# A fused two-layer encoder on one core: `wo`'s third block in a spare bank, and a new order of sums, root and keys ahead of the cross-attention

## The chip, the cores and the metric

The kernel runs on one core of a Trainium2 chip, in one launch. The metric is the device time of that core in microseconds. An engine takes its instructions in the order of its own queue; the order is fixed when the program is built. TensorE (PE) multiplies, VectorE (DVE) and ScalarE (ACT) do the element work, SyncE (SP) and GpSimd (POOL) start the transfers.

## The reference

Two layers over a sequence of 512 tokens of width 1024, in float32. Each layer is a mixer, a cross-attention to a memory of 256 tokens, and a gated feed-forward; the change touches the seam between the mixer and the cross-attention.

```
for layer in range(2):
    xn = rms_norm(x, mix_norm[layer])
    mixed = fox_diff_mixer(xn, ...)  if layer == 0 else  mlstm_mixer(xn, ...)
    x = x + mixed                                   # ends in "@ w_out"
    x = x + memory_cross_attention(rms_norm(x, xattn_norm[layer]), rms_norm(mem, mem_norm[layer]), wq, wkv, wo)
    x = x + conv_ffn(rms_norm(x, ffn_norm[layer]), ...)
return rms_norm(x, final_norm)

def memory_cross_attention(xn, memn, wq, wkv, wo):  # 4 heads of 256
    q = split_heads(xn @ wq, 4)
    k, v = jnp.split(memn @ wkv, 2, axis=-1)
    p = jax.nn.softmax((q @ k^T) * 256 ** -0.5)
    return merge_heads(p @ v) @ wo
```

## The kernel before

**Products.** Every float32 product is done in three: each operand is split into a high half (a cast on ScalarE, line 285) and a low half (a subtraction on VectorE, line 282), and TensorE adds high x high, high x low and low x high (lines 291 to 293). A weight block comes by DMA into `raw` (or another buffer) and becomes `wh`, `wl`.

**The order.** Each stage is planned by a small list planner (`Plan`): items have a priority, the items they depend on, resources they take and free, an estimated time, and optional order marks (`order`) that only say "behind that item". It writes the program in the order found, and the framework below then fixes the order on each engine. PSUM has eight banks: four "acc" banks and two rings of two, "s" (small results) and "w" (aux: weighings, transposes, first query products).

**The mixer's output projection** (`p_out`): eight blocks `m` of 128 output rows; each takes an "acc" bank, does 8 x 3 products of 512 columns against the heads' outputs (`mh`/`ml`, and in layer 0 the last heads' `ka`, `qa`), and is then added to `x` (`xadd`, line 619). `xprep` makes `xh`, `xl` of the new `x` (lines 603, 604) and adds its square to `sq` (lines 597, 598). In layer 0 two of the four "acc" banks are held at that time by the fills, so the blocks pass through the other two. In that layer `x` is loaded again for the add (`reload`).

**The fills** (`p_fill`): the first four blocks of the memory's keys are multiplied early into two "acc" banks; their results are scaled later (`keys`, line 1372) and split into `kv`.

**The queries** (`p_query`, one call for each head `h` of four) use seven products of 256 columns in place of eight (a fast two-by-two scheme). `p_forms` makes sums and differences of `x`'s parts (lines 1495 to 1498, into `kv`); the weights' sums are made partly by DMA: `sum_load` loads one part into `sa` (line 1169, SP), then an accumulating DMA on POOL adds the other (line 1170). `sa` has three buffers, so the fourth sum, head 3's, is loaded once `wl<-sa` of head 0 has been read off the first. `rest_load` loads `ra`. Inside `p_query`, `p6` makes the sum `sa + raw` on VectorE (line 1228) into `sb` or `qs`, splits it as `s2` and multiplies; `p3` adds the other half of `raw` (line 1239); `p4` splits `ra`. For heads 0 and 1 these items have priorities of their own, interleaved with the end of the output projection; `seed` copies -X into the accumulating bank (line 1214), `kept` copies intermediate results to `xe` tiles (line 1224).

**The norm of the queries** is applied in the softmax: `rsqrt_cols` sums `sq` over the partitions with eight small matmuls (line 452, into an "s" bank), and `rsqrt` takes the root's inverse in twelve small VectorE steps (lines 461 to 467). The first score needs the result as the exponential's scale. The `xe` tiles (four buffers) also hold the exponentials.

Of the kernel before, what the change touches and what calls it, by code (L numbers as in the profile page):

```python
# [17 lines left out]
P = 128  # L18
SEQ = 512
DM = 1024  # L20
KB8 = DM // P
MEM = 256
# [5 lines left out]
EPS = 1e-6  # L28
# [108 lines left out]
MM = 0.2275  # L137
# [99 lines left out]
class Builder:  # L237
# [64 lines left out]
            self.mm3(ps[:, :n], wh[:, s], wl[:, s], xh[k][:, :n], xl[k][:, :n], k == 0, k == nk - 1)  # L302
        return ps

    def p_proj(self, pl, src, xs, evac, chain, deps=(), kdeps=None, edeps=(), prio=None, n=SEQ, nk=KB8, order=None, etake=(), per=2, eorder=(), load=(), off=0):

        order = order or list(range(nk))
        st = {}
        last = None
        cuts = list(range(0, nk, per)) + ([nk - 1] if per == 2 and nk > 6 else [])  # L310
        for c, e in zip(cuts, cuts[1:] + [nk]):
            ks = order[c:e]

            def fn(c=c, ks=ks):
                if c == 0:
                    st["w"] = self.weight(src, nk * P, off)
                    st["ps"] = self.acc_bank(st["banks"][0])
                (wh, wl), (xh, xl) = st["w"], xs()
                for j, k in enumerate(ks):
                    s = slice(k * P, (k + 1) * P)  # L320
                    self.mm3(st["ps"][:, :n], wh[:, s], wl[:, s], xh[k][:, :n], xl[k][:, :n], c + j == 0, c + j == nk - 1)

            d = list(deps) if c == 0 else [last]
            for k in ks:
                d += (kdeps or {}).get(k, [])
            first = c == 0
            last = pl.add(
                fn, 3 * len(ks) * MM * n / 512, d, prio, take=("acc", "wt") if first else (), free=("wt",) if e == nk else (),
                pre=(("A", 0.12 * nk), ("D", 0.14 * nk)) if first else (), st=st,
            )  # L330
        return pl.add(lambda: evac(st["ps"]), 0, [last, *edeps], prio, take=etake, free=("acc",), chain=chain, order=eorder, load=load, st=st)

    def p_proj_tok(self, pl, src, xs, ntok, evac, deps=(), kdeps=None, edeps=(), prio=None, n=512, etake=(), ready=None, chain=None):

# [88 lines left out]
    def xs(self):  # L423
        return self.xh, self.xl

    def p_out(self, pl, src, mixed, kdeps, gain, gi, order, prio, reload=False, order0=None):

        state = {}
        done = []
        for m in range(KB8):  # L430
            e = self.p_proj(
                pl, src[m], mixed, lambda ps, m=m: self.xadd(m, ps, reload), (("D", 0.6),), kdeps=kdeps, order=order, prio=prio + m
            )
            done.append(
                pl.add(lambda m=m: self.xprep(m, gain, gi, state), 0, [e], prio + m, chain=(("A", 0.52), ("D", 0.66), ("A", 0.52)), order=[order0])
            )
        self.state = state
        self.xdone = {k: [d] for k, d in enumerate(done)}
# [167 lines left out]
    def xprep(self, k, gain, gi, state):  # L606

        if gain is not None:
            if k == 0:
                self.xh, self.xl = [None] * 8, [None] * 8  # L610
            self.xh[k] = self.til(self.xp, f"xh{k}", dtype=F32R, bufs=1)
            self.xl[k] = self.til(self.xp, f"xl{k}", dtype=F32R, bufs=1)
            self.gained(k, self.x[k][:], self.col(gain, gi * 8 + k), self.xh[k][:], self.xl[k][:])
        self.squares(k, self.x[k][:], SEQ, state)

    def xadd(self, m, ps, reload=False):
        if reload:
# [559 lines left out]
    def p_query(self, pl, layer, h, order):  # L1177
# [3 lines left out]
        st = {}  # L1181
        a1, a2 = self.t["xq"][layer, 2 * h], self.t["xq"][layer, 2 * h + 1]

        def wide(tag, raw):
            both = self.til(self.kp, tag, (P, 1088), F32R, bufs=1)
            s = st[tag] = [both[:, c : c + 512] for c in (OFF, OFF + 512)]
            self.split(*s, raw)

        def product(w, c, xs, bank, first, ks=range(4)):
            for k in ks:  # L1190
                at = slice(c + k * P, c + (k + 1) * P)
                self.mm3(st[bank][:, :256], w[0][:, at], w[1][:, at], *xs(k), first and k == 0, k == 3, True)
# [31 lines left out]
            nc.scalar.copy(st[n][:], st[bank][:, :256])  # L1224

        def p6():
            st["sb"] = self.til(mp, "qs", bufs=1) if h % 2 else self.til(self.kp, "sb", bufs=2)
            tt_(out=st["sb"][:], in0=self.sums[h][:, 512:], in1=st["raw"][:, :512], op=ALU.add)
            if h == 0:
                self.sum_load(layer, 2)  # L1230
            wide("s2", st["sb"][:])
            product(st["s2"], 0, T2, "Y", False, range(4 - (h == 0)))
# [18 lines left out]
        n = 1.42  # L1251
# [15 lines left out]
        pl, mp, fin, ends = yield sd  # L1267
# [3 lines left out]
        formed = self.formed[1:] if lead else self.formed  # L1271
        q5 = pl.add(p5, n - part, formed, p5a, take=("s", "wt"))
        q6 = pl.add(p6, n - part, [sd, *formed], p6a, order=[q5])
        if lead:
            q5 = pl.add(lambda: product(st["f1"], 512, T1, "R", True, range(3, 4)), part, [q5, *self.formed], p5_, order=[q6])
# [12 lines left out]
    def xattn(self, layer):  # L1288
        nc, t, tc = self.nc, self.t, self.tc
        with tc.tile_pool(name=f"xa{layer}", bufs=1, reuse_waits="tile") as mp:  # L1290
            self.mp = mp
            pl = Plan(self.plan, [st["banks"][0] for st in [*self.fills, *self.held]], s=2, w=0, e=4, q=2, pt=2, wt=1, hs=2)
# [13 lines left out]
            def last():  # L1306
# [5 lines left out]
            self.formed.insert(0, pl.add(  # L1312
                last, 0, self.xdone[7], 0, order=self.formed[:], take=("hs", "hs"), free=("hs", "hs")
            ))
            norm = pl.add(
                lambda state=self.state: rs.append(self.rsqrt_cols(state["sq"], SEQ, 256.0 / DM, 256.0 * EPS)), 0.4, self.xdone[7], 2.5, take=("s",), free=("s",), chain=(("D", 2.3),)
            )
            mh, ml = [None] * 8, [None] * 8
            kd = {}
            kth, ktl, vh, vl, rs = [], [], [], [], []  # L1320
            qs, qe = [None] * 4, [None] * 4
# [43 lines left out]
            for h in range(4):  # L1365
                p = 50 + 10 * h
                ke = []
                for m in (2 * h, 2 * h + 1):

                    def keys(ps, m=m, at=0):  # L1370
                        tmp = self.til(mp, "tmp", (P, MEM))
                        nc.vector.tensor_tensor(out=tmp[:], in0=ps[:, at : at + MEM], in1=self.memrb, op=ALU.mult)
                        self.split(kth[m // 4][:, m % 4, :], ktl[m // 4][:, m % 4, :], tmp[:])

                    kc = (("D", 0.34), ("A", 0.34), ("D", 0.34))
                    if m < 2 * len(self.fills):
                        st = self.fills[m // 2]
                        ke.append(
                            pl.add(
                                lambda keys=keys, st=st, m=m: keys(st["ps"], at=m % 2 * MEM), 0, [kvs], p, free=("acc",) if m % 2 else (), chain=kc, st=st,  # L1380
                                order=ke[-1:] if m % 2 else (),
                            )
                        )
                        continue
                    ke.append(
                        self.p_proj(
                            pl, t["xk"][layer, m], self.mems, keys, kc, deps=[kvs], prio=p, n=MEM, per=4, off=OFF
                        )
                    )
# [85 lines left out]
            for k in range(4):  # L1475
                last_form = pl.add(
                    lambda k=k: form(k), 0, [*used, *self.xdone[2 * k + 1]], 100 + 2 * k + 2, order=[last_form],
                    chain=(("A", 1.5), ("D", 1.4), ("A", 1.0), ("D", 1.2)) if k < 3 else (),
# [817 lines left out]
```

## Time and profile before

| | before |
|---|---|
| median of 3 runs | 1459.03 us (1458.19 to 1459.31) |
| profiled execution | 1458.72 us |
| its span | 1456.9 us, TensorE clock 0.999 |
| PE busy | 1440.6 us (99%), 9019 instructions |
| DVE busy | 1225.9 us (84%) |
| ACT busy | 985.5 us (68%) |
| POOL busy | 72.9 us (5%) |
| DMA | 190.24 MB, 131 GB/s over the span |

A row of the timeline shows the start, the duration, the engine, the line, the operation, out<-in by the program's names, and in brackets the idle time ahead of it and what ended it. Matmuls overlap: a row's duration is longer than the distance to the next start, which is the pace. The profile's line numbers are those of the kernel before; in the changed kernel they are one to five higher. The seam lies at about 220 to 335 us of the span in layer 0 and 935 to 1040 us in layer 1.

### The profile page before, as it was taken

How to read it: one execution, taken by the hardware profiler on the slowest of the kernel's cores; microseconds unless marked ns; L12 is line 12 of the kernel's file. 1: busy time of each engine (PE TensorE's matmuls, PEld its weight loads, DVE VectorE, ACT ScalarE, POOL GpSimd, SP SyncE). 2: the span in 40 equal slices, each digit the busy share in tenths (PEclk: the TensorE clock that was granted, in tenths of full speed). 3: DMA queues.
4: the chain of work that ended last, by engine and by line, in shares of the span. 5: the costliest groups of instructions: out<-in, count | busy, mean ns of one | idle time of the engine just before them, and what ended most of it. 6: DMA issues, size and time to landing. Idle time of an engine off the chain costs nothing.

```text
span 1456.9 us, 24068 instructions
## 1 busy us (share of the span) xinstructions
PE 1440.6 (99%) x9019; PEld 1277.7 (88%) x9019; DVE 1225.9 (84%) x2224; ACT 985.5 (68%) x1775; POOL 72.9 (5%) x116
## 2 busy tenths in 40 slices
PE   9999999999999999999999999999999999999998
PEld 7888787998899999999888888889988999999987
DVE  7789987867899988889669988887779998888974
ACT  7689665655677777777547665566566777777764
POOL 0001120000000000000000100000000000000000
PEclk9999999999999999999999999999999999999999
DMA  5222436652246656662233332656413666656322
GB/s 200 87 74 73 118 122 195 169 179 87 94 122 169 183 158 157 155 160 77 84 101 108 111 109 65 204 142 189 131 49 117 162 178 173 154 157 160 104 67 78
DMA packets 70628, 190.24 MB, mean 131 GB/s; under 512 B 7520, under 2 KB 7520, under 8 KB 70512
## 3 DMA queue, kind: packets, MB, share of 16 engines
q1 hardware_dynamic: 62304, 161.38, 35.0%
q0 software_dynamic: 7200, 26.22, 10.6%
q8 instruction: 70, 1.15, 0.3%
q10 hardware_dynamic: 1008, 1.12, 0.2%
q14 instruction: 46, 0.38, 0.1%
HBM read 186.56 MB, written 2.13 MB: 130 GB/s over the span
## 4 chain that ended last, share of the span: by engine, by line
PE 82%; DVE 10%; ACT 4%; issue 2%; DMA 2%; SPq 0%; POOL 0%; ACTq 0%; DVEq 0%; POOLq 0%
PE acc L291 15%; PE acc L292 14%; PE acc L293 14%; PE w L293 6%; PE w L291 6%; PE w L292 6%; PE s L293 3%; PE s L291 3%; PE s L292 3%; PE acc L352 2%; PE acc L354 2%; PE acc L353 2%; DVE wl L282 2%; DMA sa<-in_xq_dram 1%; DVE x L771 1%
## 5 line engine op out<-in xcount | busy, mean ns | idle before, releaser
L282 DVE TENSOR_TENSOR wl<-raw,wh 128x1024 fp32r<-128x1024 f32 (+3 forms) x181 | 213.9, 1182 | 41.2 <-ACT wh L285 32.4
L291 PE MATMUL acc<-xh,wh 128*128 128x256 f32 (+1 forms) x624 | 206.8, 331 | 0.2 <-ACT v L1917 0.2
L293 PE MATMUL acc<-xh,wl 128*128 128x256 f32 (+1 forms) x624 | 205.6, 329 | 0.1
L292 PE MATMUL acc<-xl,wh 128*128 128x256 f32 (+1 forms) x624 | 205.5, 329 | 0.0
L285 ACT CAST wh<-raw 128x1024 fp32r<-128x1024 f32 (+1 forms) x123 | 126.6, 1034 | 84.3 <-PE acc L292 42.9
L1676 DVE SCALAR_TENSOR_TENSOR c<-hs,vec,c 128x512 f32<-128x512 f32 x176 | 130.4, 749 | 16.0 <-ACT c L1669 14.0
L291 PEld LDWEIGHTS acc<-xh,wh 128*128 128x128 f32 x624 | 117.2, 188 | 12.1 <-ACT v L1917 0.6
L293 PEld LDWEIGHTS acc<-xh,wl 128*128 128x128 f32 x624 | 117.2, 188 | 12.0 <-DVE wl L282 0.5
L292 PEld LDWEIGHTS acc<-xl,wh 128*128 128x128 f32 x624 | 117.2, 188 | 11.5
L293 PE MATMUL w<-ah,wl 128*128 128x512 f32 x304 | 119.1, 392 | 0.0
L292 PE MATMUL w<-al,wh 128*128 128x512 f32 x304 | 118.6, 390 | 0.0
L291 PE MATMUL w<-ah,wh 128*128 128x512 f32 x304 | 118.5, 390 | 0.0
L282 DVE TENSOR_TENSOR wl<-sa,wh 128x1024 fp32r<-128x1024 f32 x52 | 63.6, 1222 | 17.0 <-ACT wh L1747 15.6
L1669 ACT ACTIVATE c<-hs,vec 128x512 f32<-128x512 f32 x88 | 71.2, 816 | 9.6 <-DVE hs L1816 8.2
L1747 ACT CAST wh<-sa 128x1024 fp32r<-128x1024 f32 x42 | 44.0, 1049 | 35.5 <-PE w L292 30.5
L293 PEld LDWEIGHTS w<-ah,wl 128*128 128x128 f32 x304 | 57.1, 188 | 12.1
L291 PEld LDWEIGHTS w<-ah,wh 128*128 128x128 f32 x304 | 57.1, 188 | 10.1 <-ACT w L1584 0.2
L292 PEld LDWEIGHTS w<-al,wh 128*128 128x128 f32 x304 | 57.1, 188 | 9.8
L282 DVE TENSOR_TENSOR s<-sb,s 128x512 fp32r<-128x512 f32 x92 | 63.1, 686 | 2.2 <-ACT s L285 0.3
L1554 ACT CAST wh<-dr 128x512 fp32r<-128x512 f32 x64 | 39.7, 621 | 34.2 <-PE w L292 32.2
L1732 POOL DMA_DIRECT2D sa<-in_up_dram x42 | 35.9, 855 | 516.5 <-DVE wl L282 184.5
L291 PE MATMUL acc<-mem,wh 128*128 128x256 f32 (+1 forms) x192 | 61.5, 320 | 0.0
(535 smaller groups left out, 4664.1 us busy)
## 6 DMA issues: line engine op xcount, KB each, us to landing
raw<-in_up_dram SPq DMA_DIRECT2D x46, 512.0 KB, 3.4
sa<-in_up_dram SPq DMA_DIRECT2D x42, 512.0 KB, 4.1
sa<-in_up_dram POOLq DMA_DIRECT2D x42, 512.0 KB, 5.5
dr<-in_down_dram SPq DMA_DIRECT2D x64, 256.0 KB, 2.8
ra<-in_up_dram SPq DMA_DIRECT2D x42, 256.0 KB, 3.1
raw<-in_xk_dram SPq DMA_DIRECT2D x16, 512.0 KB, 3.6
raw<-in_wo_dram SPq DMA_DIRECT2D x16, 512.0 KB, 3.6
raw<-in_xv_dram SPq DMA_DIRECT2D x16, 512.0 KB, 3.4
```

Of the source, the lines that this page charges most:

```text
L282: self.nc.vector.tensor_tensor(out=lo, in0=v, in1=hi.bitcast(F32), op=ALU.subtract)
L285: self.nc.scalar.copy(hi, v)
L291: mm(out, wh, xh, start=first, stop=False, skip_group_check=parts)
L292: mm(out, wh, xl, start=False, stop=False, skip_group_check=parts)
L293: mm(out, wl, xh, start=False, stop=last, skip_group_check=parts)
L352: mm(ps, xh[k][:, ts], wh[:, ws], start=(k == 0), stop=False)
L353: mm(ps, xh[k][:, ts], wl[:, ws], start=False, stop=False)
L1554: nc.scalar.copy(st["wh"][:, :cols], st[tag][:, :cols])
L1669: nc.scalar.activation(st["c_"][:, j, :], hs()[:, j, 2:514], AF.Identity, scale=self.col("cw", (layer * 3 + 2) * 44 + blk), bias=self.col( ...
L1676: nc.vector.scalar_tensor_tensor(out=c, in0=hs()[:, j, n : n + 512], scalar=w, in1=c, op0=ALU.mult, op1=ALU.add)
L1732: return add("POOL", 0.0029 * cols, lambda: nc.gpsimd.dma_start(out(), src(), accum_op=ALU.add), deps, due, (), (), 6.0)
L1747: nc.scalar.copy(s["wh"][:, :cols], raw())
```

## The change

1. `p_proj` can take a bank of another ring (`room`) and stand behind given items (`behind`). In layer 0's output projection block 2 takes a bank of "w" and stands behind the last weighing (`kdeps[3]`).
2. For the norm of the cross-attention `x`'s last square is left out of `xprep` and made in a new item `inverse`, together with the eight small matmuls and the root. The item's priority goes from 2.5 to 36.6, behind all queries, in both layers.
3. Head 2's sum goes to `qs` and head 3's to `sb` (before: head 2's to `sb`, head 3's to `qs`).
4. The keys of the fills are scaled into `xe` tiles, not `tmp`.

```diff
-    def p_proj(self, pl, src, xs, evac, ..., load=(), off=0):
+    def p_proj(self, pl, src, xs, evac, ..., load=(), off=0, room="acc", behind=()):
...
-                    st["ps"] = self.acc_bank(st["banks"][0])
+                    st["ps"] = self.acc_bank(st["banks"][0]) if room == "acc" else self.bank(room)
...
-                fn, 3 * len(ks) * MM * n / 512, d, prio, take=("acc", "wt") if first else (), free=("wt",) if e == nk else (),
-                pre=(("A", 0.12 * nk), ("D", 0.14 * nk)) if first else (), st=st,
+                fn, 3 * len(ks) * MM * n / 512, d, prio, take=(room, "wt") if first else (), free=("wt",) if e == nk else (),
+                pre=(("A", 0.12 * nk), ("D", 0.14 * nk)) if first else (), st=st, order=behind,
...
-                pl, src[m], mixed, lambda ps, m=m: self.xadd(m, ps, reload), (("D", 0.6),), kdeps=kdeps, order=order, prio=prio + m
+                pl, src[m], mixed, lambda ps, m=m: self.xadd(m, ps, reload), (("D", 0.6),), kdeps=kdeps, order=order, prio=prio + m,
+                room="w" if reload and m == 2 else "acc", behind=kdeps[3] if reload and m == 2 else (),
...
-        self.squares(k, self.x[k][:], SEQ, state)
+        if gain != "xat" or k < 7:
+            self.squares(k, self.x[k][:], SEQ, state)
...
-            st["sb"] = self.til(mp, "qs", bufs=1) if h % 2 else self.til(self.kp, "sb", bufs=2)
+            st["sb"] = self.til(mp, "qs", bufs=1) if h in (1, 2) else self.til(self.kp, "sb", bufs=2)
...
-            norm = pl.add(
-                lambda state=self.state: rs.append(self.rsqrt_cols(state["sq"], SEQ, 256.0 / DM, 256.0 * EPS)), 0.4, self.xdone[7], 2.5, take=("s",), free=("s",), chain=(("D", 2.3),)
-            )
+            def inverse(state=self.state):
+                self.squares(7, self.x[7][:], SEQ, state)
+                rs.append(self.rsqrt_cols(state["sq"], SEQ, 256.0 / DM, 256.0 * EPS))
+
+            norm = pl.add(inverse, 0.4, self.xdone[7], 36.6, take=("s",), free=("s",), chain=(("A", 0.52), ("D", 2.9)))
...
-                        tmp = self.til(mp, "tmp", (P, MEM))
+                        tmp = self.til(mp, "xe", (P, MEM), bufs=4) if m < 2 * len(self.fills) else self.til(mp, "tmp", (P, MEM))
```

TensorE in layer 0, from the last weighing's last two matmuls (`w_2628`) on. Before, with `acc_481` and `acc_510` for blocks 0 and 1 and `acc_549` for block 2:

```order
L1031 MATMUL w_2628<-pt_2333,v_1734 64x128
L1031 MATMUL w_2628<-pt_2554,v_1734 64x128
L291 MATMUL acc_481_2421<-qa_523_2637,wh_2416 128x512
L291 MATMUL acc_510_2547<-qa_523_2637,wh_2542 128x512
L292 MATMUL acc_481_2421<-qa_524_2638,wh_2416 128x512
L293 MATMUL acc_481_2421<-qa_523_2637,wl_2417 128x512
L292 MATMUL acc_510_2547<-qa_524_2638,wh_2542 128x512
L293 MATMUL acc_510_2547<-qa_523_2637,wl_2543 128x512
L291 MATMUL acc_549_2689<-mh_128,wh_2684 128x512
```

The changed kernel at the same place, where block 2 is `w_2647`:

```order
L1033 MATMUL w_2628<-pt_2333,v_1734 64x128
L1033 MATMUL w_2628<-pt_2554,v_1734 64x128
L291 MATMUL w_2647<-mh_128,wh_2642 128x512
L292 MATMUL w_2647<-ml_134,wh_2642 128x512
L293 MATMUL w_2647<-mh_128,wl_2643 128x512
L291 MATMUL w_2647<-mh_129,wh_2642 128x512
L292 MATMUL w_2647<-ml_135,wh_2642 128x512
L293 MATMUL w_2647<-mh_129,wl_2643 128x512
L291 MATMUL acc_481_2421<-qa_523_2637,wh_2416 128x512
L292 MATMUL acc_481_2421<-qa_524_2638,wh_2416 128x512
L293 MATMUL acc_481_2421<-qa_523_2637,wl_2417 128x512
L291 MATMUL acc_510_2547<-qa_523_2637,wh_2542 128x512
```

Six products of block 2 now stand between the weighing and the first products that read `qa`; the block's other 18 follow those of blocks 0 and 1.

VectorE in layer 0, in the queries, behind `x`'s last square (`sq`) or the form 3 (`hs`, `kv_534`; `kv_538` after). Before, `sb_3301` is head 2's sum, `tmp_3507` and `tmp_3511` are the first fill's keys, `z` begins the root, and head 1's low half (`s_641`, with `qs_3148`) follows eight rows on:

```order
L598 TENSOR_TENSOR sq_2681<-sq_2681,sqt_2976 128x512
L1495 TENSOR_TENSOR hs_3036<-hs_3035 128x512
L1228 TENSOR_TENSOR sb_3301<-sa_3060,pg_3261 128x512
L1496 TENSOR_TENSOR hs_3036<-hs_3035,hs_3036 128x256
L1372 TENSOR_TENSOR tmp_3507<-acc_434_2161,memrb_1758 128x256
L1497 TENSOR_TENSOR hs_3036<-hs_3035,hs_3036 128x256
L1372 TENSOR_TENSOR tmp_3511<-acc_434_2161,memrb_1758 128x256
L282 TENSOR_TENSOR kv_534_2659<-hs_3036,kv_530_2655 128x1024
L461 TENSOR_SCALAR z_3080<-s_3075 128x4
```

In the changed kernel `sb_3396` is head 3's sum, of the fourth `sa`, and `s_635` is head 1's low half:

```order
L1500 TENSOR_TENSOR hs_3047<-hs_3046 128x512
L599 TENSOR_TENSOR sq_2700<-sq_2700,sqt_3475 128x512
L1501 TENSOR_TENSOR hs_3047<-hs_3046,hs_3047 128x256
L1502 TENSOR_TENSOR hs_3047<-hs_3046,hs_3047 128x256
L282 TENSOR_TENSOR kv_538_2672<-hs_3047,kv_534_2668 128x1024
L282 TENSOR_TENSOR wl_3093<-sa_2772,wh_3092 128x1024
L282 TENSOR_TENSOR wl_3240<-pg_3237,wh_3239 128x1024
L1230 TENSOR_TENSOR sb_3396<-sa_3144,raw_3356 128x512
L282 TENSOR_TENSOR s_635_3126<-qs_3124,s_635_3126 128x512
L1241 TENSOR_TENSOR qs_3124<-qs_3124,raw_2972 128x512
```

Head 2's sum, the keys and the root have left this stretch for later places, and head 3's sum has come into it, ahead of head 1's low half. In layer 1 the same rows stand so.

More of the change, by code (lines that the diff above doesn't have):

```diff
@@ L303, in proj, with p_proj @@
         return ps
-    def p_proj(self, pl, src, xs, evac, chain, deps=(), kdeps=None, edeps=(), prio=None, n=SEQ, nk=KB8, order=None, etake=(), per=2, eorder=(), load=(), off=0):
+    def p_proj(self, pl, src, xs, evac, chain, deps=(), kdeps=None, edeps=(), prio=None, n=SEQ, nk=KB8, order=None, etake=(), per=2, eorder=(), load=(), off=0, room="acc", behind=()):
         order = order or list(range(nk))
@@ L327, in p_proj @@
             last = pl.add(
-                fn, 3 * len(ks) * MM * n / 512, d, prio, take=("acc", "wt") if first else (), free=("wt",) if e == nk else (),
-                pre=(("A", 0.12 * nk), ("D", 0.14 * nk)) if first else (), st=st,
+                fn, 3 * len(ks) * MM * n / 512, d, prio, take=(room, "wt") if first else (), free=("wt",) if e == nk else (),
+                pre=(("A", 0.12 * nk), ("D", 0.14 * nk)) if first else (), st=st, order=behind,
             )
-        return pl.add(lambda: evac(st["ps"]), 0, [last, *edeps], prio, take=etake, free=("acc",), chain=chain, order=eorder, load=load, st=st)
+        return pl.add(lambda: evac(st["ps"]), 0, [last, *edeps], prio, take=etake, free=(room,), chain=chain, order=eorder, load=load, st=st)
     def p_proj_tok(self, pl, src, xs, ntok, evac, deps=(), kdeps=None, edeps=(), prio=None, n=512, etake=(), ready=None, chain=None):
```

## The prediction

> **What bounds the kernel now.** First the page's busy shares.
>
> ```profile
> span 1456.9 us, 24068 instructions
> PE 1440.6 (99%) x9019; PEld 1277.7 (88%) x9019; DVE 1225.9 (84%) x2224; ACT 985.5 (68%) x1775; POOL 72.9 (5%) x116
> ```
>
> TensorE is busy for all but 16.3 us, so a change that neither adds nor removes products can only move TensorE's waits. The profiled execution took 1458.72 us: its span and 1.82 us around it. It lies 0.31 us below the median 1459.03. I sum against it and add the 0.31 at the end. About 0.2% (2.9 us) is what a measurement of this kernel can tell from no change.
>
> Next the windows around the places that the change touches: the end of layer 0's mixer with `wo`, the queries of layer 0's attention, those of layer 1's.
>
> ```profile
> 220.00:265.00 45.00, 43.20 (x209) 34.66 (x208) 35.19 (x51) 28.20 (x42) 2.70 (x3) 1.00 0.66 192
> 265.00:300.00 35.00, 34.56 (x297) 33.96 (x296) 26.92 (x51) 22.13 (x41) 3.40 (x4) 1.00 0.74 190
> 965.00:1000.00 35.00, 34.69 (x295) 34.11 (x294) 29.17 (x53) 23.40 (x41) 2.57 (x3) 1.00 0.75 195
> ```
>
> The second number of each row is TensorE's busy time: it idles for 1.8, 0.44 and 0.31 us, at a full clock (1.00). A busy TensorE can also be a slow one, so I read starts in its timeline. At `wo`:
>
> ```profile
> 222.10 3.00 PE L1031 MATMUL w<-pt,v 128*64 128x512 f32 x16
> 225.78 0.73 PE L291 MATMUL acc<-qa,wh 128*128 128x512 f32 x2 [0.68 <-ACT qa L285]
> 228.02 0.50 PE L291 MATMUL acc<-mh,wh 128*128 128x512 f32 x1 [0.33 <-DVE x L619]
> 228.59 0.40 PE L293 MATMUL acc<-mh,wl 128*128 128x512 f32 x1
> 233.60 0.39 PE L291 MATMUL acc<-mh,wh 128*128 128x512 f32 x1
> ...
> 222.72 0.29 DVE L805 COPY pt<-w 128x128 f32<-128x128 f32 x1 [0.83 <-ACT pt L803]
> 225.76 0.69 DVE L282 TENSOR_TENSOR qa<-w,qa 128x512 fp32r<-128x512 f32 x1 [2.75 <-ACT qa L285]
> ```
>
> From 228.59 to 233.60 lie 22 products of 512 columns: 0.2275 us each. After the last weighing TensorE waits for `qa` (0.68), then `wo`'s third block waits for a bank that `x`'s add frees (0.33). Counting starts, 30 products from the weighing's end (its row ends at 225.10; a next product starts some 0.16 before the modelled end, 0.39 less 0.2275, so at 224.94) to 233.60 need 6.82 us and took 8.66: these two waits and their restarts cost 1.84 us.
>
> **Part 1: the third block in "w", behind the last weighing.** Its weights are split earlier in both orders. Six products of finished heads (6 x 0.2275 = 1.37 us) now stand in 224.94 to 226.30; `qa`'s low half starts at 225.76 and takes 0.69, done 226.45, while the first product that reads only the high half can start at 226.30. Blocks 0 and 1 end, and the block goes on, without the bank wait. Gain up to 1.84 us; least 0, if "w"'s other buffer were still held (the copy at 222.72, the last to read it, is over by 223.0, so I take 1.84).
>
> **Part 2: the root's sums and early steps moved.**
>
> ```profile
> 269.29 0.95 PE L452 MATMUL s<-ones,sq 128*128 128x2 f32 x8
> 972.38 0.95 PE L452 MATMUL s<-ones,sq 128*128 128x2 f32 x8
> 973.19 0.36 PE L291 MATMUL w<-xh,wh 128*128 128x256 f32 x1
> 974.57 0.28 PE L293 MATMUL acc<-kv,s 128*128 128x256 f32 x1
> 975.63 0.39 PE L291 MATMUL s<-xh,s 128*128 128x256 f32 x1 [0.31 <-ACT xe L1224]
> 975.85 0.28 PE L292 MATMUL s<-xl,s 128*128 128x256 f32 x1
> ```
>
> The eight small matmuls take 0.81 us (972.38 to 973.19) and slow the next by 0.09: 0.9. They are still done, after the queries, so this is zero in sum; the twelve small VectorE steps behind them too. What they are late for is the first score's exponential, with 48 products of 0.2275 (10.9 us) between: covered. What the move can gain is the wait at 975.63: the four starts from 974.57 to 975.85 took 1.28 us, at the pace of 256 columns (half of 0.2275, 0.114) 0.46, so 0.8 is lost; layer 0 has the like at 272.53.
>
> **Part 3: which sum goes early.** Here I expect the loss. Before, VectorE's early sum is head 2's (`sb<-sa,pg`, 267.01). Now head 3's sum stands right ahead of the low half of head 1's `s2`, which TensorE needs; head 3's `sa` is the fourth in-memory sum: a load, then an accumulating load, both after `wl<-sa` of head 0 has released its buffer.
>
> ```profile
> 264.01 1.22 DVE L282 TENSOR_TENSOR wl<-sa,wh 128x1024 fp32r<-128x1024 f32 x1
> 267.01 0.68 DVE L1228 TENSOR_TENSOR sb<-sa,pg 128x512 f32<-128x512 f32 x1
> 267.61 0.42 DVE L1496 TENSOR_TENSOR hs<-hs,hs 128x256 f32<-128x256 f32 x1
> 267.95 0.42 DVE L1372 TENSOR_TENSOR tmp<-acc,memrb 128x256 f32<-128x256 f32 x1
> 268.28 0.42 DVE L1497 TENSOR_TENSOR hs<-hs,hs 128x256 f32<-128x256 f32 x1
> ...
> 265.26 0.38 SPq L1169 DMA_DIRECT2D sa<-in_xq_dram  x1
> ...
> 269.71 0.86 POOL L1170 DMA_DIRECT2D sa<-in_xq_dram  x1 [10.03 <-DMA sa<-in_xq_dram]
> ...
> DMA to landing us min/median/max: 5.5/5.5/5.5
> ```
>
> The last row is that accumulating load's: it lands at 269.71 + 5.5 = 275.2, which is 9.9 us after `wl` ends (265.23). Before, its reader stood at 280.12 and nobody waited:
>
> ```profile
> 280.12 0.68 DVE L1228 TENSOR_TENSOR qs<-sa,raw 128x512 f32<-128x512 f32 x1
> ...
> 273.31 0.69 DVE L282 TENSOR_TENSOR s<-qs,s 128x512 fp32r<-128x512 f32 x1
> ...
> 275.72 0.28 PE L293 MATMUL acc<-kv,s 128*128 128x256 f32 x1
> ```
>
> The middle row is the low half that TensorE needs (273.31); the product that reads it first is the third of head 1's `acc<-kv,s` (275.72). VectorE runs in order and does get stuck on such a load; the row to show it is head 0's sum:
>
> ```profile
> 237.20 0.69 DVE L1228 TENSOR_TENSOR sb<-sa,sa 128x512 f32<-128x512 f32 x1 [3.75 <-DMA sa<-in_xq_dram]
> ```
>
> *Layer 1*, where everything up to `wl<-sa` is unchanged:
>
> ```profile
> 966.59 1.22 DVE L282 TENSOR_TENSOR wl<-sa,wh 128x1024 fp32r<-128x1024 f32 x1
> ...
> 972.45 0.84 POOL L1170 DMA_DIRECT2D sa<-in_xq_dram  x1 [10.62 <-DMA sa<-in_xq_dram]
> ...
> DMA to landing us min/median/max: 5.4/5.4/5.4
> ...
> 976.40 0.69 DVE L282 TENSOR_TENSOR s<-qs,s 128x512 fp32r<-128x512 f32 x1
> ...
> 978.81 0.28 PE L293 MATMUL acc<-kv,s 128*128 128x256 f32 x1
> ```
>
> Landing 972.45 + 5.4 = 977.85, 10.0 after `wl`'s end (967.81). VectorE takes up the sum then, starts the low half 0.60 later (its steps of 0.68 us start 0.60 apart, as 267.61 follows 267.01) and ends it at 977.85 + 0.60 + 0.69 = 979.14. TensorE's third product starts at 979.2 instead of 978.81: 0.4 later, and the 0.9 of the root's sums is still to come: **a loss of 1.3 us** (0.4 + 0.9). Without the wait TensorE would have been there at about 977.9 and the layer would stand at 0.
>
> *Layer 0.* Part 1 brings TensorE's last `wo` product forward, and with it `x`'s last add and `wl<-sa`. Before:
>
> ```profile
> 260.57 0.39 PE L293 MATMUL acc<-qa,wl 128*128 128x512 f32 x1
> ...
> 258.06 1.22 DVE L282 TENSOR_TENSOR kv<-s,kv 128x1024 fp32r<-128x1024 f32 x1 [0.52 <-ACT kv L1498]
> ...
> 262.81 0.68 DVE L619 TENSOR_TENSOR x<-acc,x 128x512 f32<-128x512 f32 x1
> ...
> 269.81 1.23 DVE L282 TENSOR_TENSOR kv<-hs,kv 128x1024 fp32r<-128x1024 f32 x1 [0.78 <-ACT kv L1498]
> ```
>
> The add starts 1.9 us after its product's end (260.96), since VectorE is behind. Now that product ends at about 260.96 - 1.84 + 12 x 0.114 for a product of head 0 that is put ahead of its last three = 260.5; if VectorE has no arrears, the add starts right then, I take 260.7, `wl<-sa` 0.6 + 0.6 later and ends at 263.2; landing at 263.2 + 9.9 = 273.1. VectorE, rid of head 2's sum (0.60), two keys (0.33 each by their starts) and the small steps, reaches the sum at 270 to 271.5 and waits about 2 us; the low half ends at 273.1 + 1.29 = 274.4 and TensorE's third product starts at 274.5: 1.2 earlier than 275.72, less 0.9 still to come, less 0.1 for one product more done before: **a gain of 0.2 us**. With all arrears kept the landing stays at 275.2, the product starts at 276.55, and the layer loses 0.8 + 0.9 + 0.1 = 1.8. With no wait it gains at most part 1's 1.84.
>
> [...]
>
> **Small parts.** The keys of two fills use "xe" in place of "tmp" and come later; two of four "xe" buffers are then held when the second score wants one, and its exponential may wait for the first score's transposes: 0 to 0.4 us in each layer, taken as 0, since 36 products stand between in the program's order. Loads of `pg` and `ra` change places on SP's queue; both land before their readers either way: 0.
>
> **Sum.** Layer 0 -0.2, layer 1 +1.3: 1458.72 + 1.1 = 1459.8, with 0.31 for the median **1460.1 us**.
>
> **The rivals.**
> - *The wait binds in both layers as summed*: 1460.1, own range 1458.7 to 1462.0 (layer 0 from -1.0 to +1.8, "xe" 0 to 0.8). Chance 0.50.
> - *The wait is covered*: the fourth sum lands before VectorE gets there, or TensorE has other products ahead of the reader. Then part 1 stays (-1.84) and layer 1 is even: 1457.2; with the waits of 0.8 at `s<-xh,s` gone in both layers as well, 1455.6. For it: VectorE had arrears in layer 0. Against: 9.9 and 10.0 us to landing in both layers. Chance 0.25, nearly half of it more than 0.2% faster.
> - *Slower: layer 0's landing does not move.* If VectorE's arrears at 262.81 stay, because `x`'s add stands behind a weight split, part 1's 1.84 is lost at the wait: +1.8 + 1.3 = 3.1, 1462.1. It decides if the add starts later than 261.7, the middle of the two cases. For it: between 258.06 and 269.81 no row of VectorE in before has idle time. Chance 0.25, over half of it more than 0.2% slower; this holds also the case that "w" is not free in time.
>
> **How the numbers follow.** Faster by over 0.2% (below 1456.1): nearly half of 0.25 and a little for unknowns, 0.14. Slower (above 1461.95): over half of 0.25 and the top of the first case, 0.22. Within: 0.64. The range reaches from the second case's middle to a little past the third's, 1456.7 to 1462.8.
>
> **What would show it.** In the changed profile: `acc<-qa` without a wait behind the weighing and no bank wait behind it (part 1); head 3's sum on VectorE with 2 to 3 us of idle before it, put down to the DMA of `sa`, in both layers; TensorE's `acc<-kv,s` of head 1 waiting at its third product for VectorE's `s`, until 274.5 and 979.2. I am wrong if that sum shows no wait, or if TensorE's wait lies elsewhere.

## The result, and the profile after

The changed kernel took 1461.86 us in the median of 20 runs (1459.69 to 1465.39), the kernel before 1459.17 (20 runs, 1457.37 to 1461.63): slower by a ratio of 1.0020, 95% interval 1.0013 to 1.0026. Forecast were 1460.1 us in a range of 1456.7 to 1462.8. So the time lies in the range and on the side that was forecast, 1.8 us above the value. A time above 1461.95 had been given 22 in 100; the median lies just below that bound.

The profiled execution took 1463.40 us. The page's busy shares of the changed kernel, then its windows at the places shown of before:

```profile
span 1461.6 us, 24066 instructions
PE 1443.3 (99%) x9019; PEld 1281.5 (88%) x9019; DVE 1227.2 (84%) x2224; ACT 985.2 (67%) x1775; POOL 73.9 (5%) x116
...
220.00:265.00 45.00, 44.97 (x225) 36.98 (x224) 37.26 (x55) 28.87 (x44) 2.70 (x3) 1.00 0.68 199
265.00:300.00 35.00, 32.07 (x256) 31.43 (x256) 24.85 (x36) 19.92 (x36) 3.27 (x4) 0.95 0.66 174
965.00:1000.00 35.00, 33.87 (x266) 32.51 (x266) 28.70 (x41) 23.11 (x40) 2.68 (x4) 1.00 0.70 173
```

TensorE's 1.8 us of idle at `wo` are gone (first row), and 2.9 and 1.1 us of idle have come in the queries (it was 0.44 and 0.31). The second row shows something that no row of before had: a granted clock of 0.95, behind the last busy time.

To compare two executions I set the same product's start in one against the other. The programs start unevenly: the changed kernel is already 1.06 us late at 215 us, ahead of the first changed instruction, and the part runs below are 0.2 to 0.95 late there. This start belongs to no edit; taken off, layer 0's seam (215 to 335 us) is 2.1 us longer than before, layer 1's (960 to 1055 us) 1.5, and little happens elsewhere.

Part 1, in the changed kernel's timeline of TensorE: the weighing is followed at once by block 2, and the first product of `qa` has no wait (before: 0.68, then 0.33 for a bank).

```profile
223.16 3.01 PE L1033 MATMUL w<-pt,v 128*64 128x512 f32 x16
226.09 0.50 PE L291 MATMUL w<-mh,wh 128*128 128x512 f32 x1
...
227.58 0.40 PE L291 MATMUL acc<-qa,wh 128*128 128x512 f32 x1
227.82 0.39 PE L292 MATMUL acc<-qa,wh 128*128 128x512 f32 x1
```

Part 3, from VectorE, SP, POOL, the landing of POOL's load, and TensorE, in layer 0:

```profile
261.88 0.69 DVE L621 TENSOR_TENSOR x<-acc,x 128x512 f32<-128x512 f32 x1 [1.19 <-PE acc L293]
263.08 1.22 DVE L282 TENSOR_TENSOR wl<-sa,wh 128x1024 fp32r<-128x1024 f32 x1
274.49 0.69 DVE L1230 TENSOR_TENSOR sb<-sa,raw 128x512 f32<-128x512 f32 x1 [2.91 <-DMA sa<-in_xq_dram]
275.10 0.68 DVE L282 TENSOR_TENSOR s<-qs,s 128x512 fp32r<-128x512 f32 x1
...
264.33 0.38 SPq L1171 DMA_DIRECT2D sa<-in_xq_dram  x1
...
269.10 0.86 POOL L1172 DMA_DIRECT2D sa<-in_xq_dram  x1 [11.72 <-DMA sa<-in_xq_dram]
...
DMA to landing us min/median/max: 5.4/5.4/5.4
...
273.24 0.28 PE L292 MATMUL acc<-kv,s 128*128 128x256 f32 x1
275.84 0.58 PE L293 MATMUL acc<-kv,s 128*128 128x256 f32 x1 [2.32 <-DVE s L282]
276.22 0.42 PE L291 MATMUL acc<-kv,s 128*128 128x256 f32 x1
...
278.57 0.41 PE L293 MATMUL s<-xh,s 128*128 128x256 f32 x1
...
279.08 0.28 PE L293 MATMUL s<-xh,s 128*128 128x256 f32 x1
```

VectorE had no arrears this time (its add waits 1.19 for TensorE), stood idle for 2.91 us before head 3's sum, and TensorE waited 2.32 for the low half behind it. Then come rows that were not forecast: from 275.84 to 278.57 products start 0.21 apart and last 0.41, where before and after that stretch they start 0.114 to 0.12 apart and last 0.28. The windows with the granted clock (the third number from the right of a row: "PEclk") say why:

```profile
272.00:274.00 2.00, 1.52 (x14) 1.32 (x12) 0.00 (x0) 1.13 (x2) 0.00 (x0) 1.00 0.96 199
274.00:276.00 2.00, 0.16 (x1) 0.16 (x1) 1.47 (x3) 0.26 (x1) 0.00 (x0) 0.87 0.61 238
276.00:279.00 3.00, 3.00 (x15) 3.00 (x16) 1.98 (x3) 0.37 (x1) 0.84 (x1) 0.52 0.47 128
279.00:282.00 3.00, 3.00 (x27) 3.00 (x27) 1.63 (x3) 1.10 (x3) 0.00 (x0) 1.00 0.91 158
```

In 276 to 279 us TensorE is busy for all 3.00 us and gets through 15 products in place of 27: half the clock. In layer 1 the wait is shorter and the clock stays at 1.00 from 979 to 984 us (the last of these rows is the root's small matmuls, now behind the queries):

```profile
981.02 0.69 DVE L1230 TENSOR_TENSOR sb<-sa,raw 128x512 f32<-128x512 f32 x1 [2.52 <-DMA sa<-in_xq_dram]
...
982.37 0.39 PE L293 MATMUL acc<-kv,s 128*128 128x256 f32 x1 [0.81 <-DVE s L282]
...
1010.00 0.95 PE L453 MATMUL s<-ones,sq 128*128 128x2 f32 x8
```

### The profile page after: what moved, and what is told of

It is laid out like the page before. It is cut to its first block, busy times and chain, and to the rows that moved or that the text cites. A ratio compares the mean times of both kernels' runs of the same rounds, so it can differ in the third digit from the quotient of the medians.

```text
span 1461.6 us, 24066 instructions
## 1 busy us (share of the span) xinstructions
PE 1443.3 (99%) x9019; PEld 1281.5 (88%) x9019; DVE 1227.2 (84%) x2224; ACT 985.2 (67%) x1775; POOL 73.9 (5%) x116
## 4 chain that ended last, share of the span: by engine, by line
PE 83%; DVE 9%; ACT 4%; issue 2%; DMA 2%; POOL 0%; SPq 0%; ACTq 0%; POOLq 0%; DVEq 0%
PE acc L291 15%; PE acc L293 15%; PE acc L292 15%; PE w L293 6%; PE w L291 6%; PE w L292 6%; PE s L293 3%; PE s L291 3%; PE s L292 3%; PE acc L352 2%; PE acc L354 2%; PE acc L353 2%; DVE wl L282 2%; DMA sa<-in_xq_dram 1%; DVE x L773 1%
```

## The experiments

The theory: VectorE's wait for the fourth sum, and TensorE's behind it, made the kernel slower, and TensorE's idle time halves its clock for some 3 us in layer 0. The rivals: the moved root or the keys cost the time, part 1's gain is not real, or the slow products have another cause. "Time" is always against the runs of before on the same chip.

**The sums put back** (all else of the change kept):

```diff
-            st["sb"] = self.til(mp, "qs", bufs=1) if h in (1, 2) else self.til(self.kp, "sb", bufs=2)
+            st["sb"] = self.til(mp, "qs", bufs=1) if h % 2 else self.til(self.kp, "sb", bufs=2)
```

> The changed kernel with only the choice of sums put back (head 2's sum to sb, head 3's to qs). If VectorE's wait for the fourth sum is what made the change slower: no idle before head 3's sum that anybody waits for, TensorE's third product of head 1's acc<-kv,s without a wait in both layers, no drop of the clock behind it, and part 1's 1.84 us stay: 1456.4 to 1457.4 us beside a before of 1459.2. If the moved root or the keys cost the time, or if the slow products in layer 0 have another cause than the wait ahead of them: 1459 to 1461.

Time 1458.28 us (before 1458.74), ratio 0.9995 (0.9986 to 1.0004). The profile: head 1's low half has no wait in front of it, nor has the third product that reads it.

```profile
271.22 0.69 DVE L282 TENSOR_TENSOR s<-qs,s 128x512 fp32r<-128x512 f32 x1
...
273.02 0.28 PE L292 MATMUL acc<-kv,s 128*128 128x256 f32 x1
273.14 0.28 PE L293 MATMUL acc<-kv,s 128*128 128x256 f32 x1
```

Layer 0's seam is 1.2 us shorter than before, layer 1's 0.4 longer. So the choice of sums carries the whole loss. Expected were 1.8 to 2.8 us less than before; the median is 0.46 less (interval: from 2.0 less to 0.6 more), so by the times the remaining edits are worth less than part 1's 1.84.

**The sums alone**, on the kernel before (the same line, the other way):

> The kernel before with only the choice of sums changed. If the wait is the cause: VectorE waits for the fourth sum ahead of head 1's low half in both layers. In layer 0 the sum lands at 275.2, the third product starts at 276.5 in place of 275.7 (+0.8), TensorE's wait is about 1 us and its clock stays at 1.00; in layer 1 it starts at 979.2 in place of 978.8 (+0.4): 1.2 us slower than before, 1460.4. If the wait costs as much by itself as in the whole change (3.5 us in the two profiles), 1462 or more; if the sums are not the cause, within 0.3 us of before.

Time 1461.31, ratio 1.0015 (1.0006 to 1.0024). VectorE waits for the sum in both layers (2.07 and 1.68 us), TensorE for its low half:

```profile
277.06 0.69 DVE L1228 TENSOR_TENSOR sb<-sa,raw 128x512 f32<-128x512 f32 x1 [2.07 <-DMA sa<-in_xq_dram]
...
278.48 0.39 PE L293 MATMUL acc<-kv,s 128*128 128x256 f32 x1 [0.51 <-DVE s L282]
...
983.12 0.38 PE L293 MATMUL acc<-kv,s 128*128 128x256 f32 x1 [0.22 <-DVE s L282]
```

The waits are the short ones that were expected, and the clock stays up (1.00 from 274 to 279 us). Layer 1 gives the expected 0.4. Layer 0 is 2.6 us longer, not 0.8: 0.8 of it is a stall at 240.73 that comes ahead of the queries (below), 1.1 is lost up to the third product (the 0.8 that was expected, and 0.3 at a longer wait for `x`'s last add), and 0.6 goes behind it, where this profile's products start 0.118 us apart from 285 to 303 and those of before 0.113 (more on the two paces below). The time excludes that the sums are harmless.

**Part 1 alone**, on the kernel before (the edits of `p_proj` and of `p_out`, as in the diff of the change), run twice:

> The kernel before with only part 1 (the third block of wo in a bank of the weighings, behind the last one). If the six products cover the wait for qa and the bank: 1.84 us faster than before, 1457.3. If the gain is taken back at the queries, because head 0's products wait for x's last add or the sums come no earlier: 1458.5 to 1459.2.

> Part 1 alone once more, beside the next kernel. If it gives 1.8 us wherever the clock stays up: 0.9 to 1.8 us faster than before, runs with clock 0.998 (1 of 11 so far) slower by about 1.4.

Times 1457.83 and 1457.70, ratios 0.9990 (0.9981 to 0.9999) and 0.9992 (0.9983 to 1.0001). The two profiles differ: layer 0's seam is 0.5 us shorter than before in the first, 1.7 in the second. Both have a new wait of TensorE in the queries, for a weight that ScalarE casts; behind it the first profile has half clock (0.21 between starts up to 273), the second not:

```profile
270.10 0.39 PE L291 MATMUL s<-kv,wh 128*128 128x256 f32 x1 [0.89 <-ACT wh L285]
270.56 0.38 PE L292 MATMUL s<-kv,wh 128*128 128x256 f32 x1
270.78 0.28 PE L293 MATMUL s<-kv,wl 128*128 128x256 f32 x1
```

(Second profile.) The seam's 1.7 us are not the waits at `wo` alone: from 235 to 258 us every product starts 1.6 earlier than before, at 264 it is 2.6, since `x`'s last add no longer stands behind VectorE's arrears, and the new wait takes 0.9 back. Behind the seam another 0.3 is lost by 960 us, in both profiles. By the times part 1 is worth about 0.9 us, with intervals that reach from nothing to 2.8, and 1.0 in the 20 of 22 runs whose clock stays up (table below).

**The wait filled** (the changed kernel; the expectation has the filler in a free half of the bank, but it overwrites what head 1's bank held, so this kernel's queries of head 1 are not the reference's; the instructions behind it are the same), run twice:

```diff
             wide("s2", st["sb"][:])
+            if layer == 0 and h == 1:
+                for _ in range(20):
+                    nc.tensor.matmul(st["Y"][:, 256:512], st["s2"][0][:, :P], T2(0)[0], start=True, stop=True, skip_group_check=True)
             product(st["s2"], 0, T2, "Y", False, range(4 - (h == 0)))
```

> The changed kernel with 20 products of 256 columns, whose result nobody reads, ahead of head 1's acc<-kv,s in layer 0 (in the free half of its bank). They fill 2.3 us of the wait of 2.6 us. If the idle time of TensorE is what halves its clock behind the wait: the third product starts at the same time as in the changed kernel, the products behind it start 0.114 us apart and not 0.214, the clock stays at 1.00, and the time is 1.5 to 1.9 us below the changed kernel's, 1460.0 to 1460.4. If the slow products come from something else (the operand just written, the transfers of that moment): still 0.214 apart, and 0 to 0.3 us slower than the changed kernel.

The profile's TensorE and windows:

```profile
272.71 2.43 PE L1236 MATMUL acc<-kv,s 128*128 128x256 f32 x20
...
275.53 0.39 PE L293 MATMUL acc<-kv,s 128*128 128x256 f32 x1 [0.16 <-DVE s L282]
275.75 0.28 PE L291 MATMUL acc<-kv,s 128*128 128x256 f32 x1
...
276.00:279.00 3.00, 3.00 (x29) 3.00 (x28) 2.09 (x4) 0.99 (x2) 0.83 (x1) 1.00 0.55 111
```

The third product still waits for the low half, starts 0.3 later than in the changed kernel (each start less what its program was late at 215 us), and behind it the clock is 1.00 and the pace 0.114. Layer 0's seam is 0.3 us longer than before in place of 2.1. Of the 1.8 us between them, 1.5 is the half clock that went with the idle time; another 0.6 is a slower pace of the changed kernel between 284 and 302 us (below), of which this run does not show that it hangs on the wait; the later third product takes 0.3 off. The time did not follow: 1461.56, ratio 1.0018 (1.0009 to 1.0027), as slow as the changed kernel had been in its first runs.

That asked for more executions of the changed kernel, the second beside other parts, the third beside the filler:

> The changed kernel once more, beside other parts on one chip. If the idle time of 2.3 us by itself halves TensorE's clock: again a stretch of about 2.9 us with starts 0.214 apart behind head 1's third product in layer 0, granted clock about 0.5, and layer 0 about 2.1 us longer than before (without the start of the program). If the drop is a matter of chance: no such stretch, and layer 0 only 0.2 to 0.4 us longer. Layer 1 is 1.4 to 1.5 us longer either way; the time 2 to 3.5 us above before's.

> The changed kernel, now on one chip with the filler. In its 30 runs so far the mean clock was 0.997 or 0.998 in 17 (median 1462.38 us) and 0.999 or 1.000 in 13 (1460.66). If the half clock behind the wait comes and goes from run to run and costs 1.7 us: again both groups, some half of the runs each, 1.3 to 2.1 us apart. If those groups were an accident of the chips: no such split.

> The filler once more, beside the changed kernel. If the filler does away with the half clock: no run below 0.999 (11 of 11 so far), and a median like that of the changed kernel's runs with full clock, within 0.5 us, so 0.5 to 1.2 us below the changed kernel's median. If the clock is not what costs the time: the same median as the changed kernel's.

The changed kernel: 1461.73 and 1461.55, ratios 1.0019 (1.0010 to 1.0028) and 1.0018 (1.0009 to 1.0027). Both profiles show the half clock again (mean granted clock 0.997 and 0.998), with waits of 2.2 and 2.4 us, and layer 0 longer by 2.0 and 2.35. Each timed run also gives its mean granted clock, and 3.4 us at half clock are 0.001 of the span. The profiles of before and of the changed kernel also have 1.7 us at half clock at the program's end. The five profiles with a drop show a mean of 0.997 or 0.998, the nine others 0.999, so I take a run with 0.997 or 0.998 for one with a drop and a run with 0.999 or 1.000 for one without:

| kernel | runs with clock 0.997 or 0.998 | their median | runs with 0.999 or 1.000 | their median |
|---|---|---|---|---|
| changed kernel, 41 runs | 23 | 1462.11 | 18 | 1460.65 |
| with the filler, 22 runs | 0 | - | 22 | 1461.38 |
| part 1 alone, 22 runs | 2 | 1459.12 | 20 | 1457.67 |
| part 1 with the keys or the norm (below), 22 runs | 6 | 1458.86 | 16 | 1457.41 |
| before, 98 runs beside these and the other parts | 1 | - | 97 | - |

The drop comes in somewhat over half of the changed kernel's runs and costs 1.5 us there; the filler's 22 runs have none. On the shared chip the filler's median was 1460.81 (ratio 1.0015, 1.0007 to 1.0024), 0.74 below the changed kernel's, as expected for a drop in half of the runs, and its profile has layer 0 only 0.1 longer than before. But its first 11 runs, on another chip, were 0.75 higher, and its 22 runs together (1461.38) are slower than the changed kernel's 18 without a drop (1460.65); so the times alone do not settle the size. The clock does settle that the filler removes the drop.

**The norm alone and the keys alone**, on the kernel before (the edits 2 and 4 of the change):

> The kernel before with only the norm moved (last square, root's sums and root behind the queries). If the eight small matmuls are only done at another time: 0 in layer 0 and, as in the kernel with the sums put back, 0.4 us lost in layer 1, so 0 to 0.8 us slower than before. If the move shortens the queries by the time that head 1's and form 3's steps no longer wait behind the root's small steps on VectorE (as the two kernels with part 1 differ by 0.64 in layer 0): 0.2 to 0.6 us faster.

> The kernel before with only the fills' keys in xe. If the second score's exponential is covered: within 0.3 us of before, in the profile as in the time. If it waits for the first score's transposes: 0.4 us or more lost between 310 and 335 us, and the same in layer 1.

Norm: 1458.53, ratio 1.0001 (0.9992 to 1.0010); its profile is shorter than before by 1.2 us in layer 0 and 0.4 in layer 1, which the time does not bear out. The 1.2 come at `x`'s last add, ahead of the root's old place: head 0's sum waited only 0.27 for its load there (before: 3.75), and VectorE had no arrears. Keys: 1458.73, ratio 0.9998 (0.9990 to 1.0007). Neither can be told from nothing, and neither explains the loss. The keys' profile has 1.6 us more in layer 0: 1.1 at a stall at 240 us and 0.3 at `x`'s last add, both ahead of the place that the keys can touch, and 0.3 by the slower pace between 291 and 302. The kernel with the sums alone has it too, and shows its cause, VectorE stuck on head 0's sum with `x`'s add behind it, so that the bank comes late:

```profile
239.28 0.69 DVE L1228 TENSOR_TENSOR sb<-sa,sa 128x512 f32<-128x512 f32 x1 [4.88 <-DMA sa<-in_xq_dram]
239.89 0.69 DVE L619 TENSOR_TENSOR x<-acc,x 128x512 f32<-128x512 f32 x1
```

In before's profile the same wait was 3.75 and cost TensorE nothing; in the keys' it was 5.20. So the landing of that load differs by some 5 us between profiles whose order up to there is the same, and a difference of a microsecond in a single profile can be no more than that. With part 1 the add stands ahead of that sum, and no profile of a kernel with part 1 has the stall.

**Part 1 with the keys, and part 1 with the norm** (the latter the version that the runs pointed to):

> The kernel before with part 1 and the keys. Part 1 alone gained 0.53 in the profile of its layer 0, with a stretch of half clock behind a wait of 0.87 us at 269.5 that cost about 1.4. If that stretch is a matter of chance or of where VectorE and ScalarE stand, which the keys change: no such stretch, 1.8 us faster than before. If part 1 always pays for it: 0.5 us faster.

> The version the runs point to: part 1 and the moved norm, with the sums and the keys as before. If the parts add up as in the profiles (part 1 -1.8 in layer 0 at full clock; the norm alone -0.4 in layer 1): 1.8 to 2.2 us faster than before, and 0.3 to 0.5 faster than part 1 alone. If the norm only shifts the waits once part 1 is in: the same as part 1 alone.

Keys: 1457.54, ratio 0.9993 (0.9984 to 1.0002), layer 0 shorter by 1.6 us at full clock, as part 1 alone (three of its 11 runs had a clock of 0.998). Norm: 1457.74, ratio 0.9991 (0.9982 to 1.0000): the same as part 1 alone. Its profile fell on an execution with half clock, behind waits of 0.77 and 0.72 us that stand one product apart:

```profile
268.38 0.39 PE L291 MATMUL s<-kv,wh 128*128 128x256 f32 x1 [0.77 <-ACT kv L1503]
268.60 0.28 PE L291 MATMUL acc<-kv,s 128*128 128x256 f32 x1
269.60 0.44 PE L291 MATMUL s<-kv,wh 128*128 128x256 f32 x1 [0.72 <-ACT wh L285]
269.84 0.41 PE L292 MATMUL s<-kv,wh 128*128 128x256 f32 x1
...
270.00:273.00 3.00, 3.00 (x16) 3.00 (x15) 2.97 (x4) 1.83 (x5) 0.00 (x0) 0.50 1.01 168
```

Three of its 11 runs had a clock of 0.998 (median 1458.89, the other eight 1457.43). All versions with part 1 and the old choice of sums lie 0.5 to 1.2 us under before; none is told from another.

## Why the prediction was right, and where a step was off

- *Part 1*: right in mechanism, and nearly in size. The waits of 0.68 and 0.33 are gone, and in every profile with part 1 the products from 235 to 258 us start 1.6 us earlier (less what the program was late), where 1.84 was forecast. That part 1 alone shortens layer 0 by 1.7 in a profile at full clock is near 1.84 by luck: 1.0 more is won at `x`'s last add and 0.9 lost at a new wait.
- *The head start reaches the add*: right. Less the 1.06 us that the program was late, `x`'s last add starts at 260.8 (forecast 260.7) and `wl<-sa` ends at 263.2 (263.2). The third rival, arrears on VectorE, fell.
- *The fourth sum binds in both layers*: right. Less the same 1.06, POOL's load lands at 273.4 (forecast 273.1) and TensorE's third product starts at 274.8 (274.5); in layer 1, less 3.26, at 979.1 (979.2). With the sums put back, the waits and the loss go. The rival of a covered wait fell with it. From the end of `wl<-sa` (264.30) to the sum's start (274.49, the moment of landing) it was 10.2 us, where 9.9 was forecast. (In the prediction's rows it is 10.0 in layer 0 too, 275.2 less 265.23, and not 9.9.)
- *Layer 1's size*: 1.3 forecast, 1.5, 1.3 and 1.0 in three profiles.
- *Layer 0's size*: the term that was mis-sized. Forecast was a gain of 0.2; three profiles show losses of 2.1, 2.0 and 2.35. The steps behind the third product were taken at the full pace of before. At the wait the clock fell to half for 3.4 us: from 275.84 to 279.08 lie 15 steps, 3.24 us in place of 1.71, so 1.5 is lost; the two groups of runs differ by 1.5 too. The wait itself was 0.3 longer than forecast, which took the gain of 0.2 away. The other 0.6 is a pace of 0.1177 us in place of 0.1133 between 284 and 302 us, which no run took apart (in the second profile of the changed kernel it holds only from 291 on). So layer 0 came out of the range that the first rival gave it, -1.0 to +1.8. That the time lies within the whole range all the same is luck: its upper end was made for arrears of VectorE, which did not come. In the runs whose clock stayed up the median was 1460.65, half a microsecond from the forecast 1460.1; in the others 1462.11.
- *The keys and the order of `pg` and `ra`*: nothing that a time could show, as forecast; *the moved root*: the same, and the wait at `s<-xh,s` that it might have removed is still 0.31 in layer 1 of the changed kernel.

Open is what sets that pace: the kernel with the sums put back, which has no such wait, runs the same stretch at 0.1177 too; the one with the filler runs it at 0.1133 in both profiles, part 1 alone in one of two.

## What to carry to other kernels

An instruction that waited for a transfer held up what stood behind it on its engine: a sum without urgency was put one row ahead of an operand that TensorE needs, VectorE waited 2.91 us for its load and TensorE 2.32 behind that. The sums alone cost 2.6 us, more than the 0.9 that part 1 alone had gained, while the page's busy shares hardly moved (TensorE 99% and VectorE 84% in both, ScalarE 68% and 67%). When a tag or a buffer is given to another step, look at where the new order puts that step, and price it by its transfer's landing (here 10.2 us behind the end of `wl<-sa`), not by its own duration (0.69). And price a wait of TensorE by its length plus what the clock does behind it: here a wait of 2.3 us cost 1.5 more in over half of the runs. Splitting a wait need not help: the two waits of 0.77 and 0.72 us, one product apart, had half clock behind them as well.

## What the hardware showed that was not expected

The granted clock halved at waits of TensorE of 0.7 to 2.4 us. In the changed kernel it fell at waits of 2.2 to 2.4 us in three of three profiles, and in 23 of its 41 runs. In part 1 alone it fell behind 0.87 us in the first profile and not behind 0.89, for the same weight, in the second, and in 2 of the 22 runs. In the profile of part 1 with the norm it fell behind 0.77 and 0.72 us, one product apart. At layer 1's wait of 0.81 us in the changed kernel's first profile it stayed at 1.00. So neither the kernel nor the length of the wait decides alone, and what else does is not shown.

The half clock lasted 3.41 us in the changed kernel's first profile, from 275.50 to 278.91. By an estimate from the clocks of the windows it was 3.4 us in part 1 with the norm too (0.94, 0.50 and 0.97 over 268 to 270, 270 to 273 and 273 to 276 us), and in the first profile of part 1 alone (0.72 over 268 to 274). It did not begin at a fixed place of the wait: 0.34 ahead of the wait's end (275.84) in the changed kernel's first profile, and, by the same 0.94, at about 269.8 in part 1 with the norm, some 0.2 behind the end of the second wait (269.60). In the 3.41 us ahead of the drop TensorE was busy for 1.43 in the changed kernel's first profile.

Products of 256 columns ran at one of two paces for long stretches, 0.1133 or 0.1177 us, at a granted clock of 1.00, in kernels with and without the wait; over the queries that makes 0.6 us. No run here tells what chooses between them.
